# Fixed slots in VectorE's pinned order for the x differences, w1 sums and split sums of superblocks 1 and 2

## The chip, the cores and the metric

The kernel runs on one core of one Trainium2 chip. The metric is the device time of one execution in microseconds (us). The median of several is given. A profile's span is about 1.8 us shorter than the time of the same execution.

## The reference, cut to what matters

```python
# x: [8, 1024, 1024], w1: [1024, 4096], w2: [4096, 1024], all float32
h = x @ w1
h = 0.5 * h * (1 + np.tanh(np.sqrt(2 / np.pi) * (h + 0.044715 * h ** 3)))
return (h @ w2).astype(np.float32)
```

## The kernel before: what the change touches

The 8192 rows of x are worked on in eight superblocks (sb) of 1024. Each of the two matmuls is a Strassen product: seven block products, numbered 1 to 7, on sums and differences of blocks, which VectorE makes. Superblocks 0 and 1 make the weight sums ("made"), and superblock 1 stores them in DRAM; superblocks 2 to 7 load them, but for the first quad of w1, which superblock 2 makes itself before the change. A *column* is 128 columns of a block of w1, of which the first matmul has 16; a *quad* is four of them, and its five sums are made together. Products 6 and 7 of the second matmul have a second level of splitting from superblock 2 on; its weight sums ("split sums", tensor `in_d`) are made in superblock 1.

A framework schedules the instructions. It is free to reorder an engine's instructions where data allow it, by a model of time. An instruction that is *pinned* has an edge behind the instruction that was traced just before it on its engine, so it cannot be moved ahead of that one.

```python
def tt(out, in0, in1, op, pin=False):          # all VectorE sums come from here (one line in the profile)
    i = nc.vector.tensor_tensor(out=out, in0=in0, in1=in1, op=op)
    if pin:
        tc.keep_in_program_order(i)

# ... XOps.make: five differences of x blocks, not pinned
tt(self[m][:, :, cols], self.blocks[u][:, :, cols], self.blocks[v][:, :, cols], SUB)

# ... matmul2_made (second matmul of superblocks 0 and 1); a step (m, q) is product m, row block q: 16 matmuls
def add(m, q):                                  # weight sum for product m, all pinned
    u, op, v = B_TERMS[m]
    t = sums[m][q]
    tt(t, raw[u][q], raw[v][q], op, True)
    # ... stored in superblock 1

start(4)
for q in range(NI // QC):
    add(4, q)
for q, ps in product2(g, 4, pieces(4), pb, True, True):
    u[q] = temp()
    nc.vector.tensor_copy(out=u[q], in_=ps)
# ... the loads of w2; steps = products 2, 5, 1, 7, 3, 6, four steps each
for i in range(2):
    prepare(i)                                  # pinned weight sum, pinned operand difference `gc`
for i, (m, q, banks, first, _, _, post) in enumerate(steps):
    prepare(i + 2)
    if first:
        banks.append(psum())
    matmuls2(banks[q], ops[i], pieces(m), first)
    post(q)                                     # pinned sums of the PSUM results
    if (m, q) == (2, 1) and sb == 0:
        xb = x_cast(sb + 1, at[1])
    if (m, q) == (5, NQ - 1):
        blocks = x_transpose(xb, load_in_order) # DMA transposes of the next superblock's x
    if sb and q == NQ - 1 and m in (1, 3):
        split_inner({1: 7, 3: 6}[m], pieces({1: 7, 3: 6}[m]))
return at["last"], blocks

# ... after each second matmul, in the main loop
xs = XOps(blocks)
xs.make(5, 1, 2, 7, 6)
```

The operand differences (tile `gc`) of products 1, 2, 5, 6, 7 are `g - g`; products 3 and 4 need none. Tiles `u` are a pool of 26 buffers that holds weights, sums, x blocks and x differences alike.

## Time and profile before

| | before |
|---|---|
| median time | 1585.52 us |
| span of the profile | 1583.6 us |
| PE busy | 1550.8 us (98%) |
| first matmul of sb 1 (448 matmuls) | 96.9 us |
| second matmul of sb 0 (448 matmuls) | 110.4 us |
| second matmul of sb 1 (448 matmuls) | 99.2 us |

In the profile's lines PE is TensorE, DVE VectorE, ACT ScalarE, POOL GpSimd and SPq the issuing of SyncE's DMAs; `ps` is a bank of PSUM.

The stage times are differences of start times in TensorE's timeline below (122.51 to 232.87, and so on). Undisturbed, 448 matmuls of 128x512 take 96.7 us, 0.216 us each, so the second matmul of superblock 0 loses 13.7 us.

TensorE's waits in the kernel before: the tile written, the engine and tile waited for, then us in total, times, longest.

```profile
PE ps L624 <- DVE gc L112: 12.8, 4, 8.6
PE ps L624 <- DVE u L112: 3.8, 2, 1.9
PE ps L299 <- DVE tmp L112: 3.1, 5, 1.5
PE ps L573 <- DMA u<-in_d: 2.4, 2, 1.8
...
```

TensorE's timeline before, second matmul of superblock 0, then the start of that of superblock 1 (start, duration, engine and line, what, number; in brackets the idle time before it and what ended that). L299 is the first matmul, L624 the second.

```profile
122.51 13.97 PE L624 MATMUL ps<-u,g 128*128 128x512 f16 x64 [1.91 <-DVE u L112]
138.40 51.97 PE L624 MATMUL ps<-u,gc 128*128 128x512 f16 x240 [1.92 <-DVE gc L112]
199.02 6.38 PE L624 MATMUL ps<-u,gc 128*128 128x512 f16 x16 [8.64 <-DVE gc L112]
205.24 13.98 PE L624 MATMUL ps<-u,g 128*128 128x512 f16 x64
...
331.64 13.97 PE L624 MATMUL ps<-u,g 128*128 128x512 f16 x64 [1.91 <-DVE u L112]
347.53 48.52 PE L624 MATMUL ps<-u,gc 128*128 128x512 f16 x224 [1.92 <-DVE gc L112]
```

Read the third line: after 8.64 us of idleness 16 matmuls take 6.38 us, where 64 undisturbed ones (next line) take 13.98. For most of them half of the clock is missing. VectorE's timeline before shows why:

```profile
181.79 1.22 DVE L112 TENSOR_TENSOR gc<-g,g 128x2048 f16<-128x2048 f16 x1
194.87 1.22 DVE L112 TENSOR_TENSOR u<-u 128x2048 f16<-128x2048 f16 x1 [11.86 <-DMA u<-xb]
196.01 0.68 DVE L112 TENSOR_TENSOR tmp<-tmp,ps 128x512 f32<-128x512 f32 x1
196.61 1.22 DVE L112 TENSOR_TENSOR u<-u 128x2048 f16<-128x2048 f16 x1
197.75 1.22 DVE L112 TENSOR_TENSOR gc<-g,g 128x2048 f16<-128x2048 f16 x1
```

The transposes that it waits for, in SyncE's timeline before:

```profile
169.24 24.12 SPq L122 DMA_TRANSPOSE u<-xb  x16
```

The `u<-u` at 194.87 is an x difference, which nobody needs before 233. The framework put it ahead of the `gc` of product 7, row block 3 (the prediction says column 3); it orders by its model of time, in which the transposes had presumably landed (the model's times were not looked at). On the chip they had not, and VectorE stood 11.86 us with everything else behind it.

Granted clock before, by windows (start:end, length, then busy time and instructions of PE, PEld, DVE, ACT, POOL, then PEclk, DMA share and GB/s):

```profile
199.00:202.00 3.00, 2.98 (x8) 1.05 (x9) 3.00 (x4) 0.00 (x0) 0.54 (x1) 0.50 0.11 15
...
205.00:208.00 3.00, 3.00 (x15) 1.37 (x14) 3.00 (x4) 0.00 (x0) 0.14 (x1) 1.00 1.01 344
```

The clock is 0.50 just after the stall and full again by 205 us.

### The profile page before, as it was taken

Reading aid. Unit: us, or ns where it says so; the run is one execution under the profiler, and the core shown is the slowest. Engines: PE = TensorE matmul, PEld = TensorE weight load, DVE = VectorE, ACT = ScalarE, POOL = GpSimd, SP = SyncE. Lnnn points to the kernel's source line nnn. Section 1 sums busy time; section 2 is a strip of 40 time slices with the busy share of each in tenths; the row PEclk is TensorE's granted clock in tenths of the full one; section 3 lists DMA queues with packets and bytes.
Section 4 is the critical chain, followed back from the end, with each engine's and each line's share of the span. In section 5 each row is a group of like instructions: output and inputs, shape, how many; then the busy total and the mean of one; then the engine's idle time right before and its main releaser. Section 6 shows DMA issues by size and latency. Waiting matters only on the chain.

```text
span 1583.6 us, 20425 instructions
## 1 busy us (share of the span) xinstructions
PE 1550.8 (98%) x7838; PEld 768.8 (49%) x7838; DVE 1011.6 (64%) x1273; ACT 474.6 (30%) x794; POOL 193.8 (12%) x280
## 2 busy tenths in 40 slices
PE   8999899999999999999999999999999999999998
PEld 4444344444444455444554445544555445544455
DVE  5865667768955566555675557656475556655564
ACT  6644004420044211441124410344103430044200
POOL 1241010212400013000220001200112001200000
PEclk9999999999999999999999999999999999999999
DMA  9999764875994567735686446955469545663154
GB/s 311 340 323 330 210 206 158 288 214 171 334 319 131 188 237 266 253 93 199 252 295 217 132 163 244 350 164 189 158 239 365 143 168 199 242 243 133 54 222 177
DMA packets 165778, 353.16 MB, mean 223 GB/s; under 512 B 72752, under 2 KB 78896, under 8 KB 164784
## 3 DMA queue, kind: packets, MB, share of 16 engines
q1 hardware_dynamic: 148240, 283.69, 51.7%
q0 software_dynamic: 17440, 68.17, 13.1%
q8 instruction: 61, 1.00, 0.3%
q14 instruction: 37, 0.30, 0.1%
HBM read 277.35 MB, written 89.13 MB: 231 GB/s over the span
## 4 chain that ended last, share of the span: by engine, by line
PE 87%; DMA 6%; DVE 3%; SPq 2%; issue 1%; ACT 0%; POOL 0%; DVEq 0%; ACTq 0%
PE ps L299 47%; PE ps L624 35%; PE ps L573 6%; SPq L122 2%; DVE u L112 2%; DMA raw_d<-u 2%; DMA u<-w_d 2%; DMA gc<-in_w_dram 1%; DVE gc L112 1%; DVE tmp L112 1%; DMA u<-in_d 0%; DMA u<-in_x_dram 0%; ACT u L149 0%; ACT g L309 0%; DMA u<-xb 0%
## 5 line engine op out<-in xcount | busy, mean ns | idle before, releaser
L299 PE MATMUL ps<-u 128*128 128x512 f16 x3584 | 776.0, 379 | 4.7 <-DVE tmp L112 3.1
L112 DVE TENSOR_TENSOR tmp<-tmp,ps 128x512 f32<-128x512 f32 x564 | 386.7, 686 | 315.8 <-ACT tmp L364 117.3
L299 PEld LDWEIGHTS <-u 128*128 128x128 f16 x3584 | 350.5, 98 | 428.0 <-issue 5.2
L624 PE MATMUL ps<-u,gc 128*128 128x512 f16 x1792 | 392.5, 381 | 12.8 <-DVE gc L112 12.8
L624 PEld LDWEIGHTS <-gc 128*128 128x128 f16 x1792 | 175.8, 98 | 227.1 <-DVE gc L112 14.7
L309 ACT ACTIVATE g<-tmp 128x512 f16<-128x512 f32 x256 | 161.2, 630 | 296.5 <-DVE tmp L112 296.3
L624 PE MATMUL ps<-u,g 128*128 128x512 f16 x1024 | 223.8, 379 | 3.8 <-DVE u L112 3.8
L112 DVE TENSOR_TENSOR u<-u 128x2048 f16<-128x2048 f16 (+2 forms) x159 | 166.0, 1078 | 25.5 <-ACT u L261 12.2
L309 ACT ACTIVATE g<-ps 128x512 f16<-128x512 f32 x256 | 151.8, 596 | 90.0 <-PE ps L299 89.7
L624 PEld LDWEIGHTS <-g 128*128 128x128 f16 x1024 | 100.2, 98 | 123.7 <-issue 4.4
L112 DVE TENSOR_TENSOR u<-u,ps 128x512 f32<-128x512 f32 x160 | 106.6, 681 | 83.1 <-ACT tmp L675 37.9
L396 POOL DMA_DIRECT2D out_dram<-tmp x64 | 35.1, 549 | 818.7 <-ACT tmp L668 626.6
L112 DVE TENSOR_TENSOR gc<-g,g 128x2048 f16<-128x2048 f16 x112 | 133.2, 1220 | 2.5 <-PE ps L624 2.5
L573 PE MATMUL ps<-u,gc 128*128 128x256 f16 x960 | 109.8, 273 | 1.3 <-DMA u<-in_d 0.6
L573 PEld LDWEIGHTS <-gc 128*128 128x128 f16 x960 | 93.7, 98 | 13.4 <-issue 1.6
L364 ACT COPY tmp<-ps 128x512 f32<-128x512 f32 x128 | 72.9, 570 | 85.5 <-PE ps L299 85.4
L112 DVE TENSOR_TENSOR gc<-u 128x2048 f16<-128x2048 f16 x60 | 73.1, 1219 | 39.3 <-PE ps L624 39.3
L112 DVE TENSOR_TENSOR tmp<-ps,tmp 128x512 f32<-128x512 f32 x128 | 88.4, 690 | 6.3 <-PE ps L299 1.4
L112 DVE TENSOR_TENSOR u<-tmp,ps 128x512 f32<-128x512 f32 x24 | 16.5, 688 | 74.7 <-PE ps L624 65.4
L668 ACT COPY tmp<-ps 128x512 f32<-128x512 f32 x24 | 14.1, 587 | 151.9 <-PE ps L624 151.9
L112 DVE TENSOR_TENSOR u<-g,g 128x2048 f16<-128x2048 f16 x48 | 59.5, 1279 | 0.0
L449 ACT COPY tmp<-ps 128x512 f32<-128x512 f32 x16 | 9.4, 586 | 158.8 <-PE ps L624 158.8
(34 smaller groups left out, 363.1 us busy)
## 6 DMA issues: line engine op xcount, KB each, us to landing
u<-w_d SPq DMA_DIRECT2D x187, 512.0 KB, 7.9
u<-raw_d SPq DMA_DIRECT2D x130, 512.0 KB, 7.1
u<-in_d SPq DMA_DIRECT2D x84, 512.0 KB, 8.0
gc<-in_w_dram SPq DMA_DIRECT2D x48, 512.0 KB, 6.6
raw_d<-u SPq DMA_DIRECT2D x32, 512.0 KB, 9.5
out_dram<-tmp POOLq DMA_DIRECT2D x64, 256.0 KB, 3.2
w_d<-u POOLq DMA_DIRECT2D x32, 512.0 KB, 6.6
xb<-in_x_dram POOLq DMA_DIRECT2D x56, 256.0 KB, 11.6
```

The costliest lines, as they stand in the source:

```text
L112: i = nc.vector.tensor_tensor(out=out, in0=in0, in1=in1, op=op)
L122: return tc.keep_in_program_order(nc.sync.dma_start(out=out, in_=in_, **kw))
L299: nc.tensor.matmul(bank, lhsT=ops[m][:, k, cs], rhs=xs[m][:, k, :], start=(first and k == 0), stop=(k == KH - 1), skip_group_check=not first,)
L309: gelu_last[0] = nc.scalar.activation(out=g[b][:, c, :], in_=src, func=GELU)
L364: nc.scalar.copy(out=v, in_=pb)
L396: return queue.dma_start(out=out2[r0:r0 + P, o0:o0 + OH], in_=src)
L449: nc.scalar.copy(out=c, in_=ps)
L573: nc.tensor.matmul(bank[:, i * HO:(i + 1) * HO], lhsT=t[:, c, i * P:(i + 1) * P], rhs=y[j][:, c, :], start=(first and i == 0 and c == 0), ...
L624: nc.tensor.matmul(bank, lhsT=a[:, c, :], rhs=pieces[c // QC][:, c % QC, :], start=(first and c == 0), stop=(c == NI - 1), skip_group_chec ...
L668: nc.scalar.copy(out=c21, in_=ps)
```

## The change

Work that VectorE does in the second matmul for the *next* superblock gets fixed, pinned places ("slots") behind given steps, at places where it should not hold up anything urgent. The table `FILL` says how many entries of the list `fill` follow each step, for superblock 0 and superblock 1.

```diff
+FILL = (
+    {(3, 2): 1, (3, 3): 2, (6, 0): 2, (6, 1): 1, (6, 2): 2, (6, 3): 2},
+    {(7, 2): 1, (7, 3): 1, (3, 0): 2, (3, 1): 3, (3, 2): 1, (3, 3): 2, (6, 0): 1, (6, 1): 1, (6, 2): 2, (6, 3): 5},
+)
 ...
-            if sb > 2 or (sb == 2 and q):
+            if sb > 1:                                      # sb 2 loads its first w1 quad too
 ...
-                quad = MadeQuad(q, sb == 0, sb == (1 if q else 2))
+                quad = MadeQuad(q, sb == 0, sb == 1)
 ...
+            if sb == 0 and c < 2:                           # start: sums of w1 columns 1 and 2, 3
+                for m in SUMS:                              # behind `s` of column c
+                    quads[0].sum(m, more[c], True)
 ...
-            tt(t, raw[u][q], raw[v][q], op, True)
+            tt(t, raw[u][q], raw[v][q], op, m != 4)         # m = 4 sums no longer pinned
 ...
+        fill = [lambda m=m: xs.make(m, pin=True) for m in (5, 1, 2, 7, 6)]
+        if sb:
+            split = [...]                                   # 7 calls of split_inner each for m = 7, 6
+            fill = split[0] + fill + split[1]
+        else:
+            fill += [lambda m=m: quad.sum(m) for m in SUMS]
 ...
             if (m, q) == (5, NQ - 1):
-                blocks = x_transpose(xb, load_in_order)
-            if sb and q == NQ - 1 and m in (1, 3):
-                split_inner({1: 7, 3: 6}[m], pieces({1: 7, 3: 6}[m]))
+                xs = XOps(x_transpose(xb, load_in_order))
+            if (m, q) == (3, 1) and sb == 0:
+                quad = MadeQuad(0, False, True)
+            if (m, q) == (6, 0) and sb:
+                quad = load_ops(w1_d[0], raw_d[0], ORDER, KH, QW)
+            for _ in range(FILL[sb].get((m, q), 0)):
+                fill.pop(0)()
+        while fill:
+            fill.pop(0)()
```

## The prediction

> **What bounds the kernel now.** TensorE: the table of busy time gives PE 1550.8 of 1583.6 us (98%); in the chain 448 matmuls of 128x512 take 96.7 us (0.216 each). A superblock needs two such stages. In the chain, superblock 1's second matmul takes 101.3 us (329.7 to 431.0), superblock 0's 112.4 (120.6 to 233.0). PE idles 33 us in all, so more than 2% (31.7 us) is out of reach.
>
> **The large loss.** The waits of TensorE show "gc from DVE" 12.8 us, the longest 8.6. In the timeline, VectorE stands 11.86 us (to 194.9) at an x difference `u<-u` that waits for the DMA transposes of x (`u<-xb`, issued 169.2 to 193.4). Behind it in its queue stands the `gc` operand of product 7, column 3; PE runs dry at 190.4 and resumes at 199.02. Its next 15 matmuls start 0.43 us apart: the 144 matmuls after the stall take 34.0 us where 31.1 is normal, 2.9 more. The Trainium skill, "TensorE: Matmul & The Clock Gate", Part 1, says that the clock falls to half after about 3.4 us of idleness; the trace agrees. Cost: 8.6 + 2.9 = 11.5 us.
>
> **What the change does.** (a) In superblock 0 the five x differences (1.14 us each, start to start) come after steps (3,2) to (6,0), about 204 us without the stall, when the transposes have been done for 10 us; product 7's operands are no longer behind them. Gain 11.5. (b) The m=4 weight sums lose their pin. Now they are forced behind the last `tmp` op of the first matmul, and PE waits 1.9 us for the first at 120.7 and again at 329.7 (`u` from DVE, 3.8 in 2 times). VectorE has gaps of about 1.2 us there and the raw weights have landed, so they can float forward: gain 0 to 3.8, I count 3. (c) At the start the sums of w1 column 1 go behind `s` of column 0; at 22.0 VectorE waited for a GpSimd cast before four sums, PE idle 1.5 us: gain about 1 (the start is DMA-bound, share 0.95). (d) In superblock 1, split sums (two of 0.65 us) have slots; five calls, three with sums (3.9 us), follow the last post (6,3). Then `u` of superblock 2's first column is ready about 5.3 us after PE starts, where the fifth product needs it at 3.45: loss up to 1.9; into superblock 1, 0.2. (e) Superblock 2 loads quad 0: 5 VectorE sums less, off the path.
> Unchanged: 1.9 us waits before product 2.
>
> **Sum.** 1585.5 - 11.5 - 3 - 1 + 2 = 1572 us. Range 1566 to 1578.
>
> **What would show it.** (a) VectorE's wait on `u<-xb` and PE's 8.6 us vanish; granted clock in 200 to 220 is 1.00; superblock 1's first matmul starts near 220 instead of 233. (b) PE's waits on DVE `u` at 120 and 330 vanish. (c) First columns end about 1 us earlier. (d) A PE wait for DVE `tmp` up to 2 us starts superblock 2.
>
> **What would make it wrong.** The pinned order may block VectorE on a buffer or DMA (w1 reloads or split stores late while 26 buffers are full) ahead of a `gc` operand: a stall over 3.4 us also costs the clock. The scheduler may place the m=4 sums no earlier, or ahead of a late cast. DMA may be too busy at the start of superblock 2, now earlier.
>
> Chances: faster 0.01, within 2% 0.96, slower 0.03.

## The result, and the profile after

The kernel after takes 1569.61 us in the median (1568.87 to 1572.08, 4 runs), the kernel before 1585.52. The ratio is 0.9903, with a 95% interval of 0.9886 to 0.9920. Ratios here are the mean time of one kernel's runs over that of the other's in the same rounds, so they are not quite the ratio of the medians quoted. Predicted were 1572 us and a range of 1566 to 1578: right.

TensorE's waits after:

```profile
PE ps L640 <- DVE gc L116: 3.8, 2, 1.9
PE ps L589 <- DMA u<-in_d: 2.4, 1, 2.4
...
PE ps L303 <- DVE tmp L116: 1.1, 1, 1.1
```

TensorE's timeline after (L303 is now the first matmul, L640 the second):

```profile
117.79 13.98 PE L640 MATMUL ps<-u,g 128*128 128x512 f16 x64
133.68 55.43 PE L640 MATMUL ps<-u,gc 128*128 128x512 f16 x256 [1.92 <-DVE gc L116]
...
216.57 96.99 PE L303 MATMUL ps<-u 128*128 128x512 f16 x448
313.40 13.98 PE L640 MATMUL ps<-u,g 128*128 128x512 f16 x64
329.30 55.43 PE L640 MATMUL ps<-u,gc 128*128 128x512 f16 x256 [1.92 <-DVE gc L116]
```

The 8.64 us wait, the slow 16 matmuls and both 1.91 us waits on `u` are gone. The 1.92 us waits at product 2 stay. The transposes are no faster than before, only nothing urgent stands behind them now. SyncE's timeline after:

```profile
163.11 26.80 SPq L126 DMA_TRANSPOSE u<-xb  x16
```

VectorE's timeline after shows the `gc` of product 7, row block 3 (197.75 before), and then the first x difference, which now has no wait in front of it:

```profile
180.53 1.22 DVE L116 TENSOR_TENSOR gc<-g,g 128x2048 f16<-128x2048 f16 x1
...
193.16 1.22 DVE L116 TENSOR_TENSOR u<-u 128x2048 f16<-128x2048 f16 x1
```

It also shows the first m=4 sum between two `tmp` operations of the first matmul, 6 us before its product starts at 117.79:

```profile
110.94 0.69 DVE L116 TENSOR_TENSOR tmp<-tmp,ps 128x512 f32<-128x512 f32 x1 [0.41 <-PE ps L303]
111.54 1.22 DVE L116 TENSOR_TENSOR u<-u 128x2048 f16<-128x2048 f16 x1
112.79 0.69 DVE L116 TENSOR_TENSOR tmp<-tmp,ps 128x512 f32<-128x512 f32 x1
```

The 16.5 us between the two spans, stage by stage, from the start times in the timelines:

| stretch | before | after | difference |
|---|---|---|---|
| start to the end of sb 0's first matmul | 120.60 | 117.79 | -2.8 |
| wait for the m=4 sum, sb 0 | 1.91 | 0 | -1.9 |
| second matmul of sb 0 | 110.36 | 98.78 | -11.6 |
| first matmul of sb 1 | 96.86 | 96.83 | 0.0 |
| wait for the m=4 sum, sb 1 | 1.91 | 0 | -1.9 |
| second matmul of sb 1 | 99.24 | 98.79 | -0.4 |
| first matmul of sb 2 | 96.69 | 97.14 | +0.4 |
| from there to the last second matmul | 952.54 | 952.54 | 0.0 |
| last second matmul to the end | 103.5 | 105.2 | +1.7 |

The last line was not foreseen, and it lies in code that did not change. In the last superblock TensorE waits for `u<-in_d` in both kernels, in the kernel before:

```profile
1523.49 1.92 PE L573 MATMUL ps<-u 128*128 128x256 f16 x16 [1.78 <-DMA u<-in_d]
1525.25 3.71 PE L573 MATMUL ps<-u,gc 128*128 128x256 f16 x32
1529.59 1.92 PE L573 MATMUL ps<-u,gc 128*128 128x256 f16 x16 [0.63 <-DMA u<-in_d]
```

and in the kernel after:

```profile
1505.92 3.53 PE L589 MATMUL ps<-u 128*128 128x256 f16 x16 [2.44 <-DMA u<-in_d]
1509.28 5.40 PE L589 MATMUL ps<-u,gc 128*128 128x256 f16 x48
```

Both wait 2.4 us, the kernel before in two pieces. But in the kernel after the 16 matmuls behind the wait take 3.53 us instead of 1.92: the windows of the trace give a granted clock of 0.50 in 1506 to 1508. That the second piece is missing may be a consequence: slower matmuls leave its load more time.

### The profile page after: what moved, and what is told of

The parts are those of the page before. It is cut to its first block, busy times and chain, and to the rows that moved or that the text cites. A ratio compares the mean times of both kernels' runs of the same rounds, so it can differ in the third digit from the quotient of the medians.

```text
span 1567.1 us, 20432 instructions
## 1 busy us (share of the span) xinstructions
PE 1548.4 (99%) x7838; PEld 768.1 (49%) x7838; DVE 1003.9 (64%) x1268; ACT 473.4 (30%) x794; POOL 196.1 (13%) x280
## 4 chain that ended last, share of the span: by engine, by line
PE 92%; DMA 4%; DVE 2%; issue 1%; SPq 0%; POOL 0%; ACT 0%; DVEq 0%; POOLq 0%
PE ps L303 48%; PE ps L640 39%; PE ps L589 6%; DMA u<-w_d 2%; DMA gc<-in_w_dram 2%; DVE u L116 1%; DVE gc L116 0%; SPq L126 0%; DVE tmp L116 0%; DMA u<-in_d 0%; DMA u<-in_x_dram 0%; POOL u L129 0%; ACT u L191 0%; ACT tmp L684 0%; SPq L398 0%
## 5 line engine op out<-in xcount | busy, mean ns | idle before, releaser
L303 PE MATMUL ps<-u 128*128 128x512 f16 x3584 | 776.1, 379 | 2.9 <-DVE u L116 1.5
L303 PEld LDWEIGHTS <-u 128*128 128x128 f16 x3584 | 350.6, 98 | 426.2 <-issue 3.7
L640 PE MATMUL ps<-u,gc 128*128 128x512 f16 x1792 | 389.4, 379 | 3.8 <-DVE gc L116 3.8
L640 PEld LDWEIGHTS <-gc 128*128 128x128 f16 x1792 | 175.3, 98 | 215.7 <-DVE gc L116 4.8
L640 PE MATMUL ps<-u,g 128*128 128x512 f16 x1024 | 223.6, 379 | 0.0
L116 DVE TENSOR_TENSOR u<-u 128x2048 f16<-128x2048 f16 (+2 forms) x154 | 159.0, 1063 | 13.3 <-ACT u L265 11.9
L640 PEld LDWEIGHTS <-g 128*128 128x128 f16 x1024 | 100.1, 98 | 119.6
L363 ACT COPY tmp<-ps 128x512 f32<-128x512 f32 x128 | 72.9, 570 | 85.8 <-PE ps L303 85.6
L116 DVE TENSOR_TENSOR u<-tmp,ps 128x512 f32<-128x512 f32 x24 | 16.5, 688 | 74.7 <-PE ps L640 65.0
L684 ACT COPY tmp<-ps 128x512 f32<-128x512 f32 x24 | 14.1, 586 | 151.9 <-PE ps L640 151.9
L691 ACT COPY tmp<-ps 128x512 f32<-128x512 f32 x24 | 14.1, 586 | 133.5 <-PE ps L640 132.7
```

The lines of the kernel that those rows point to most:

```text
L303: nc.tensor.matmul(bank, lhsT=ops[m][:, k, cs], rhs=xs[m][:, k, :], start=(first and k == 0), stop=(k == KH - 1), skip_group_check=not first,)
L363: nc.scalar.copy(out=v, in_=pb)
L640: nc.tensor.matmul(bank, lhsT=a[:, c, :], rhs=pieces[c // QC][:, c % QC, :], start=(first and c == 0), stop=(c == NI - 1), skip_group_chec ...
L684: nc.scalar.copy(out=c21, in_=ps)
L691: nc.scalar.copy(out=c12, in_=ps)
```

## The experiments

All on the chip, each timed beside the kernel before in the same rounds (median 1585.76, 1585.33 and 1584.98 us in the three sessions). Every result was correct.

**1. Only the x differences pinned, in the kernel before.**

```diff
 ...
+            for k in {(3, 2): (5,), (3, 3): (1, 2), (6, 0): (7, 6)}.get((m, q), ()) if sb == 0 else ():
+                xs.make(k, pin=True)
 ...
```

> The kernel before with one part of the change alone: the five x differences of superblock 1 are pinned behind steps (3,2), (3,3), (6,0). Theory (the stall is a matter of the order in VectorE's queue, 8.6 us of wait and 2.9 us of half clock): about 11.5 us less than before, 1574, ratio 0.9927; the 8.6 us PE wait on gc and the 11.9 us VectorE wait on u<-xb are gone, the two 1.9 us PE waits on u remain. Rival (the transposes themselves come late, and the gain came from the quad sums and split sums that moved): no gain, 1585.

Measured: 1575.98 us, ratio 0.9943 (0.9930 to 0.9955), so 9 to 10 us and not 11.5. The stall is gone as the theory has it: TensorE runs 256 matmuls of the second matmul without a break. But superblock 1 now starts with a wait that the kernel before did not have. TensorE's timeline:

```profile
138.25 55.43 PE L626 MATMUL ps<-u,gc 128*128 128x512 f16 x256 [1.92 <-DVE gc L112]
...
223.22 97.02 PE L299 MATMUL ps<-u 128*128 128x512 f16 x448 [1.92 <-DVE u L112]
```

The rival falls: the transposes were as late as ever (in that trace issued from 169.39 to 193.72) and the time was won all the same. The missing 1.9 us is the new wait. VectorE's timeline shows why: the five w1 sums of superblock 1 now stand behind the last PSUM sum of product 6.

```profile
221.34 0.69 DVE L112 TENSOR_TENSOR u<-u,ps 128x512 f32<-128x512 f32 x1 [2.76 <-PE ps L626]
221.94 5.76 DVE L112 TENSOR_TENSOR u<-u 128x2048 f16<-128x2048 f16 x5
```

They are pinned, in the kernel before too. There the instruction traced just before them was an x difference that was free to move, and they moved ahead with it; here it is that last PSUM sum. So pinning one group moved another that was pinned behind it. Experiment 5 tests whether these five cost the 1.9 us.

**2. The kernel after, with the x differences in early slots.**

```diff
-    {(3, 2): 1, (3, 3): 2, (6, 0): 2, (6, 1): 1, (6, 2): 2, (6, 3): 2},
+    {(7, 0): 1, (7, 1): 1, (7, 2): 1, (7, 3): 2, (6, 1): 1, (6, 2): 2, (6, 3): 2},
```

> The kernel after, with the same pins but the x differences of superblock 1 in early slots, behind (7,0), (7,1), (7,2), (7,3), so that the first stands ahead of the operand of product 7, column 3, as the scheduler had it before. Theory: the stall comes back, PE waits 8 to 9 us on gc, the clock halves for some 15 matmuls, 11 to 12 us more than after: 1581. Rival (pinning as such, or the other parts of the change, made the gain): stays at 1570.

Measured: 1579.42 us, ratio 0.9964; about 10 us more than after. TensorE's timeline:

```profile
193.46 5.06 PE L640 MATMUL ps<-u,gc 128*128 128x512 f16 x16 [6.93 <-DVE gc L116]
```

The stall comes back, a little shorter than expected in the profiled run (6.9 us, and 1.4 more for the clock, as these 16 matmuls take 5.06 us and 3.63 at full clock in experiment 7; the stage takes 107.3 us, against 98.8); that run was the fastest of the five. Against the stall, pins alone gain nothing: where they put the instruction decides. The rival falls.

**3. The m=4 sums pinned again, in the kernel after.**

```diff
-            tt(t, raw[u][q], raw[v][q], op, m != 4)
+            tt(t, raw[u][q], raw[v][q], op, True)
```

> The kernel after with the m=4 weight sums pinned again. Theory: PE waits 1.9 us for u at the start of both made second matmuls again, 3.8 us more: 1573.4, ratio to before 0.9924. Rival (the change gained nothing there, the wait only moved to product 2): 1569.6.

Measured: 1574.44 us, ratio 0.9930, so 4 to 5 us more than after. Both waits are back in TensorE's waits, and the one before product 2 is as long as in the kernel after:

```profile
PE ps L640 <- DVE gc L116: 3.8, 2, 1.9
PE ps L640 <- DVE u L116: 3.8, 2, 1.9
```

The surplus over 3.8 us is in the start, at least in the profiled run: its first matmul ends 1.6 us later than in the profile of after, which varies from run to run (next experiment).

**4. The start as before, in the kernel after.** The sums of w1 columns 1 to 3 are traced ahead of the first matmul again, unpinned.

```diff
-                more.append(quads[0].load_cols(c, n))
+                cs = quads[0].load_cols(c, n)
+                for m in SUMS:
+                    quads[0].sum(m, cs)
 ...
-            if sb == 0 and c < 2:
-                for m in SUMS:
-                    quads[0].sum(m, more[c], True)
```

> The kernel after with the sums of the first w1 columns as before the change (unpinned, traced ahead of the first matmul). Theory: the first matmul of superblock 0 ends 2.5 us later again (after gained 2.8 us between the start and there), 1572. Rival (that stretch is bound by the loads of w1, and the 2.8 us is how the loads fell): no change, 1569.6.

Measured: 1570.26 us, ratio 0.9906: hardly different from after, against both clean answers. The profile has both halves. The first matmul ends at 120.52, 2.7 us later than in the profile of after; in return the last superblock's wait (2.13 and 0.68 us) cost no clock, which gives some 1.3 us back. And 2.7 was luck: over the nine profiles with the new start, that matmul ends at 117.8 to 119.7 us, mean 118.7; over the four with the old start at 119.9 to 120.6, mean 120.4 (each is the start of product 4, less its wait). By the profiles the new start is worth about 1.6 us; the timed medians, 1570.26 and 1569.61, differ by 0.65 and lie in each other's ranges, so the times do not show it. Why it varies more was not tested; the chain of the kernel after runs through the loads of w1 up to 39 us.

**5. The w1 sums of superblock 1 without slots, in the kernel after.** They follow the last step, pinned.

```diff
-    {(3, 2): 1, (3, 3): 2, (6, 0): 2, (6, 1): 1, (6, 2): 2, (6, 3): 2},
+    {(3, 2): 1, (3, 3): 2, (6, 0): 2},
```

> The kernel after with the slots of the x differences kept and those of the five quad sums of superblock 1 given up (they follow the last step, pinned). Theory (this is what the x slots alone lacked, where PE waited 1.9 us for u at the start of superblock 1): a PE wait of 1.9 us there, 1571. Rival (the 1.9 us had another cause): 1569.2, no wait.

Measured: 1571.05 us, ratio 0.9910. TensorE's timeline has the expected wait at the start of superblock 1:

```profile
219.50 97.03 PE L303 MATMUL ps<-u 128*128 128x512 f16 x448 [1.92 <-DVE u L116]
```

The total, 1.4 us above after, lies within the noise; the wait in the trace decides. So the slots of the w1 sums carry 1.9 us of the 11.6. They do not win time over the kernel before: they keep the x slots from losing it again.

**6. The x differences unpinned, in the kernel after.** Traced behind the last step, with the slots of the other work kept.

```diff
-    {(3, 2): 1, (3, 3): 2, (6, 0): 2, (6, 1): 1, (6, 2): 2, (6, 3): 2},
+    {(6, 1): 1, (6, 2): 2, (6, 3): 2},
 ...
+        if sb == 0:
+            xs.make(5, 1, 2, 7, 6)
```

> The kernel after with the x differences of superblock 1 unpinned and traced behind the last step. In the order of the built program the scheduler puts them behind the last post of product 6 this time, with two quad sums: seven operations of 1.14 us. Theory (a queue position is what costs): no stall in product 7, but PE waits at the second product of superblock 1 for the first x difference and later for u, 2 to 6 us in all: 1572 to 1576. Rival (without pins the scheduler brings the old stall back): PE waits 8.6 us on gc in product 7, 1581.

Measured: 1574.20 us, ratio 0.9929, 4 to 5 us more than after. TensorE's timeline:

```profile
216.92 1.03 PE L303 MATMUL ps<-u 128*128 128x512 f16 x4
221.27 97.68 PE L303 MATMUL ps<-u 128*128 128x512 f16 x444 [3.32 <-DVE u L116]
```

No stall in product 7, but 3.3 us at the second product of superblock 1, which needs the first x difference, and 1.7 us of reduced clock behind it (the first matmul of superblock 1 takes 101.9 us instead of 96.8). An unpinned instruction is too early in one version of a kernel and too late in the next.

**7. TensorE kept busy during the stall, in the kernel before.**

```diff
+            if sb == 0 and (m, q) == (7, 3):
+                for _ in range(40):
+                    tc.keep_in_program_order(nc.tensor.matmul(
+                        banks[q], lhsT=idle[:, :P], rhs=idle, start=False, stop=True, skip_group_check=True))
```

> The kernel before with 40 matmuls of a tile of zeros (adding zero to the bank of product 7, column 3, so the result stays right) ahead of the stalled product, to fill TensorE's 8.6 us of waiting at 0.216 us each. Nothing becomes ready earlier. Theory (the slow pace after the stall is the clock falling for idleness): the 15 matmuls after it run at 0.216 us, 2.9 us less than before: 1582.5, ratio 0.9982. Rival (they were slow because of the VectorE and DMA work that starts at the same moment): 1585 or more.

Measured: 1587.01 us, ratio 1.0012 (0.9999 to 1.0024). The total contradicts the expectation; the place does not. TensorE's timeline:

```profile
189.48 8.80 PE L517 MATMUL ps<-idle 128*128 128x512 f16 x40
199.41 3.63 PE L628 MATMUL ps<-u,gc 128*128 128x512 f16 x16 [1.14 <-DVE gc L112]
202.88 13.98 PE L628 MATMUL ps<-u,g 128*128 128x512 f16 x64
219.26 15.67 PE L628 MATMUL ps<-u,gc 128*128 128x512 f16 x64 [2.41 <-DVE gc L112]
```

The 16 matmuls behind the filled gap take 3.63 us instead of 6.38, with the same VectorE and DMA work starting beside them: the slow pace was the clock, and idleness lowers it. The rival falls. What was won is lost at product 6. The added instructions shifted the framework's order so that two w1 sums stand ahead of three `gc`, and VectorE's timeline shows them waiting for their loads:

```profile
211.39 1.22 DVE L112 TENSOR_TENSOR u<-u 128x2048 f16<-128x2048 f16 x1 [4.03 <-DMA u<-raw_d]
213.98 1.23 DVE L112 TENSOR_TENSOR u<-u 128x2048 f16<-128x2048 f16 x1 [1.36 <-DMA u<-raw_d]
...
217.99 3.49 DVE L112 TENSOR_TENSOR gc<-g,g 128x2048 f16<-128x2048 f16 x3
```

It is the same fault once more: work for later, placed early on a model of when its load lands. It costs 2.4 us of waiting and, again, 1.7 us of clock.

**8. The kernel after, again.** Unchanged, beside the next three.

> The kernel after once more, unchanged, beside the next three on one chip, for the spread of its executions. Expected 1569.6, 1568.5 to 1572.5; in the profile the first matmul of superblock 0 ends between 117.8 and 119.4 us (it varied that much in three kernels that share this start) and the last superblock has its one DMA wait of about 2.4 us, with or without half clock behind it (1.7 us).

Measured: 1569.11 us (1568.27 to 1569.83), ratio 0.9898. In its profile sb 0's first matmul ends at 118.70, and the wait at the end is 2.41 us with half clock behind it, all as expected.

**9. The operand differences of product 2 made earlier.** The 1.92 us waits that the change left: VectorE makes the first `gc` of product 2 behind the four PSUM copies of product 4.

```diff
+        ops = {i: operand2(g, 2, i, True) for i in range(2)}
         for q, ps in product2(g, 4, pieces(4), pb, True, True):
 ...
-        ops = {}
-        for i in range(2):
-            prepare(i)
```

> The kernel after with the first two operand differences of product 2 traced ahead of product 4, so that they no longer stand behind its four PSUM copies in VectorE's queue. Theory (the last two 1.9 us waits of PE on gc are queue order too): both vanish, 3.8 us less than after: 1566. Rival (the time goes into waiting for the copies or the operands of columns 2 and 3 instead): the waits move one or two columns on, 1569.

Measured: 1564.51 us, ratio 0.9869, 4.6 us less than after in the same session, 0.8 more than the two waits; where that lies was not looked for. Both waits are gone and did not move on; the waits of TensorE name `gc` no more.

**10. Stores of block 21 in the last superblock on GpSimd's queue.**

```diff
-        queue = nc.gpsimd if sb < NSB - 1 else nc.sync
+        queue = nc.gpsimd if sb < NSB - 1 or b == "21" else nc.sync
```

> The kernel after with the four output stores of block 21 in the last superblock on GpSimd's queue, as in all other superblocks, and no longer on SyncE's, where the loads u<-in_d stand behind them. Theory (those loads come late because SyncE waits for the copies that the stores read; the wait then halves the clock in some executions): the 2.4 us PE wait on u<-in_d goes, and the half clock behind it: 2.4 to 4.2 us less than after, 1566 to 1567, and less spread. Rival (the loads wait for free buffers, whatever the queue): same as after.

Measured: 1567.02 us (1566.85 to 1567.51), ratio 0.9886, 2.1 us less than after in the same session and the smaller spread that was expected, but a little less gain than expected. The wait on `u<-in_d` is gone from TensorE's waits, so the rival falls; in the profiles the stretch from the last second matmul to the end took 101.4 us against 105.3 in experiment 8. The profiled run gained 3.0 us in its span in spite of a start 1.0 us later (119.65). The timed runs gained less than the stretch of the profile; as no trace exists of them, which part was missing there stays open.

**11. Both, and the split sums of superblock 1 spread.**

```diff
-    {..., (3, 3): 2, (6, 0): 1, (6, 1): 1, (6, 2): 2, (6, 3): 5},
+    {..., (3, 3): 3, (6, 0): 2, (6, 1): 2, (6, 2): 2, (6, 3): 2},
```

> Both of these, and the split sums of superblock 1 spread so that only two calls follow the last post of its second matmul (0.4 us PE wait at the start of superblock 2). If the gains add: 3.8 + 3 to 4.2 + 0.4, so 1562 to 1563; ratio to before 0.9855. Rival: what is gained before superblock 2 is lost again to loads that come late there (DMA share near 1), 1565 to 1567.

Measured: 1561.21 us (1560.74 to 1562.24), ratio 0.9849 (0.9834 to 0.9864): the fastest version, 24.1 us below before and 7.9 us below after in the same session. The gains add, to within 0.8: 4.6 + 2.1 + 0.4 (the last expected, not measured alone) is 7.1. TensorE's waits in it, all of them:

```profile
PE ps L303 <- DVE tmp L116: 2.0, 2, 1.8
PE ps L303 <- DVE u L116: 1.5, 1, 1.5
PE ps L239 <- DVE warm L703: 1.2, 1, 1.2
```

## Why the prediction was right, point by point

- **(a) The stall, predicted -11.5, measured -11.6** in the second matmul of superblock 0. Experiments 1 and 2 take it away and bring it back by the position of the x differences alone. What I had not seen is that the x slots alone give 1.9 us of it away again at the start of superblock 1; the slots of the w1 sums, which I booked as a cost of 0.2 us, prevent that (experiments 1 and 5). The margin was mis-sized as well: I put the first x difference at about 204 us, 10 us after the transposes. VectorE came to it at 193.16, 3.2 us after the last of them was issued (163.11 + 26.80); ScalarE copies out the results of product 3, so no PSUM sum held VectorE back there. That it had no wait was closer than I thought.
- **The clock part of it, predicted 2.9 us, measured 2.8 by the start times:** shown to be due to idleness by experiment 7. The Trainium skill, "TensorE: Matmul & The Clock Gate", Part 1, has the half clock; the trace has 0.50 in 199 to 202.
- **(b) The m=4 sums, predicted -3, measured -3.8** (two waits of 1.9 us). Experiment 3 brings both back.
- **(c) The start, predicted -1, measured -2.8** in the one profile. Over all profiles it is about -1.6, and the timed runs do not resolve it. The mechanism held in the profiles: TensorE's wait for `tmp` near 25 us, 1.5 to 1.8 us in the four with the old start, is in none of the nine with the new one, though some of these wait up to 1.8 us near 44 us. The size in the single profile was luck.
- **(d) The split sums behind the last post, predicted up to +1.9, measured +0.4.** The mis-sized term: I assumed that TensorE runs column 0's products in the written order and so meets its fifth product at 3.45 us. The built program places the first products of column 1 ahead of it. TensorE ran 23 matmuls (5.0 us) before it had to wait.
- **Not in the sum at all: +1.7 at the end.** A DMA wait of 2.4 us in the last superblock, outside the changed code, was followed by half clock in the profile of after and not in that of before. The last section shows what decided that.
- **(e) Superblock 2's first quad loaded:** VectorE has 1268 instructions instead of 1273, and no stage shows a gain or loss from it.
- The Trainium skill, same page, "Architectural detail: the array is 16× 32×32, not 1× 128×128", says that VectorE's queue is strictly first in, first out. The trace agrees: with VectorE idle for 11.86 us at one instruction, nothing behind it ran.

The terms of the prediction sum to -13.5; measured were -15.9 by the medians and -16.5 by the spans. Terms (b) and (c) were too small, (d) too big, and the end took 1.7 back.

## What to carry to other kernels

Where TensorE is 98% busy, look for the few long waits, and ask of each not what was late but what stood in the queue behind the late thing. An instruction that prepares for later work, and waits for a DMA, belongs behind the last urgent operation of its engine but ahead of the moment it is needed; if a scheduler with a model of time places it, any edit can move it to the wrong side, so pin it. Count a stall of about 2 us or more on TensorE with its clock: in these profiles nine such waits cost another 1.4 to 2.8 us each, and four waits of 2.0 to 2.4 us cost nothing more (last section). A pin holds an instruction only to the one traced before it: when that one is moved or pinned, look where those behind it go.

## What the Trainium skill lacked or had wrong

- "TensorE: Matmul & The Clock Gate", Part 1, gives about 3.4 us of idleness for the fall to half clock. Here measured waits of 1.96, 2.32, 2.36, 2.41 and 2.44 us were followed by reduced clock, while others of 2.01, 2.04, 2.13 and 2.42 us were not, nor, once the clock was full, any of 1.92 or less. The traces explain which. They hold each change of the granted clock, and in each of the 13 profiles the changes lie whole multiples of 3.413 us apart (in after at 3.97, 1505.84, 1509.25 and 1563.86: 440, 1 and 16 of them). Cut the profiles into such stretches: the clock fell after all nine stretches at full clock in which TensorE idled 1.96 us or more, and after none with 1.92 or less. The waits of 2.01, 2.04, 2.13 and 2.42 us lay across two stretches, with at most 1.72 us in either; the 1.78 and 0.63 us in the last superblock of before left at most 1.31 in one. The page's remark that the window is free-running fits this, but a length of 3.4 us for the idleness needed does not. (Matmul ends are modelled in the profile, so a wait can be off by a few tenths.)
- How much idleness within one stretch is enough is on no page. Here the half clock lasted 10.24 us for the wait of 8.64 us, 6.83 for that of 6.93, and 3.41 for each of the other seven, whatever their length. So 8.64 us of waiting cost 2.8 us more, 6.93 cost 1.4, 3.32 cost 1.7, 2.44 cost 1.6 (112 matmuls of the last superblock took 14.1 us after it, 12.5 with no wait in experiment 10).
- "DMA: Bandwidth & Descriptors", "Latency and other measured facts", gives 261 GB/s for DMA transposes and 350 to 400 when contiguous. Here 16 transposes of a 1024x1024 block of two-byte elements, 2.1 MB, took 24.1 us from the first issue to the last, which is 87 GB/s, in the first half with other transfers beside them. In the window 182 to 192 us, in the second half, all queues together moved 102 GB/s at a DMA share of 0.45. No run varied the transposes, so the reason is open.
